# Residual sums of the second token half in small tiles, scaled from there; two low parts made on GpSimd

## The chip, the core and the metric

The kernel runs on one core of a Trainium2 chip. The metric is the device time of one execution in microseconds (us). The core has a matrix engine (PE, with its weight loads as PEld), a vector engine (DVE), a scalar engine (ACT) and a general engine (POOL, GpSimd); SP only issues DMAs here. Each works through its own queue in order; semaphores tie the queues together.

## The reference, cut to what matters

One decoder layer for 1024 new tokens of one sequence and 8 single tokens of running sequences, 1032 tokens in all, width 1024. The two recurrent mixers are left out here; o_a and y are their outputs, 1024 wide each, and gate and val have 2816 columns each:

```python
h = rmsnorm(x, w['norm1_w'])
proj = h @ w['w_in']
...
x = x + jnp.concatenate([o_a, y], axis=-1) @ w['w_out']
h = rmsnorm(x, w['norm2_w'])
gate, val = jnp.split(h @ w['w_up'], 2, axis=-1)
gate, buf_f_new = causal_dwconv(gate, buf_f, w['ffn_conv_w'], w['ffn_conv_b'])
x = x + (jax.nn.silu(gate) * val) @ w['w_down']
```

All of it is float32. The change concerns the sum behind `w_out`, the second norm's weight and the first products with `w_up`.

## The kernel before

Everything is kept transposed: features on the 128 partitions, tokens along the row. A float32 product is made from three reduced-precision ones: each operand is split into a high part (a cast to the type fp32r, on ACT) and a low part (the operand less its high part, usually on DVE), and PE adds high x high, high x low and low x high.

**Output projection** (`out_job`, L1199). The 1032 tokens stand in two halves (`hf`) of 516, each in two quarters (`c`) of 258 (`QW`). The result is `xh[hf][m]`, eight rows of tiles m of 128 features; `xpair` holds two of them in one tile. Jobs named o8 and o12 do one half of the contraction for all tokens, then o0 and o4 the other, first for half 0, then for half 1 (`o0.*.1`, `o4.*.1`). Each product is 12 matmuls into a PSUM bank, emptied by an addition on DVE (L1234). In the last job of a half (`last`, the o4 jobs) the sum is complete. `final` (L1244) then stores it to DRAM (`x1_d`, for the last residual), squares it on ACT and adds the square on POOL to `rst`, from which the second norm's factor comes. For half 1, `weigh` (L1256) multiplies the finished row of tiles, in place, by the norm's weight `n2`. It is put off by 28 ticks; a tick is one matmul traced. The token's own factor is applied to half 1 only behind the up projection (L1498, L1507).

**Sets** (`set_of`, L1328). The up projection uses seven products instead of eight on quarters of the operands (the Strassen-Winograd form): weights in feature halves 1 and 2 and in gate and value columns, activations a1, b1 (quarters 0 and 1, rows 0 to 3) and a2, b2 (quarters 0 and 1, rows 4 to 7). The seven operands p1 to p7 of a half are its set: p1 = a1, p2 = a2, p4 = b2, p5 = b1 - b2, p6 = p5 less a1, p3 = p6 plus a2, p7 = a1 - b1. `comb` (L1356) makes the sums in two pieces on DVE or POOL. `put` (L1345) casts the high part on ACT (L1352) and subtracts for the low part on DVE (L1353). Plain operands are taken in two pieces of 128x516, sums in one of 128x1032.

**Up projection** (`ups`, L1526; `Up`, L1445). For each of 22 blocks of 128 columns there are 14 products of 12 matmuls: in block 0 the seven of half 0, then the seven of half 1 (`FIRST`); in the others alternating (`ORDER`). Products p1, p7 and p3 (named ua) use a pool of three PSUM banks; the others (ub) use one of four. Their evictions are p1 L1464 and p5 L1472 (ACT), p6 L1468, p2 L1484, p4 L1492, p7 L1476 and p3 L1504 (DVE). p4's waits until p7 has been added up; p3's until POOL has done L1477 and L1478 behind p7. `set_norm` sums the squares over the partitions with a matmul (n2ms) and works out the factor (`rstd_of`, L736 to L739). Weight sums of the next block are made by POOL (L1422), its splits are L1441 (ACT) and L1442 (DVE).

**What sets the order.** PE runs in the order of the code (`manual_schedule` for PE). Everything else is traced between PE's matmuls: `after(n, f)` runs f n ticks later and `spread(pieces, n)` one piece every n ticks. The queues of the other engines are ordered by the planner of the tile framework: an instruction traced earlier goes first among those that it reckons ready. A tile that is allocated takes a buffer of its tag when one is free. The tags of `TAGS` (L42) that matter are hT (16 buffers of 1032), big (10 of 1056), x5 (5) and us (10 of 258). During the output projection hT holds its inputs; big holds the eight residual tiles. The tag us holds the squares, the evicted products and the norm's scratch.

The lists of the sets are made from these lines:

```python
after(4, lambda: spread(set_of(1), 4))
after(93, lambda: (set_norm(1, 0), set_norm(1, 1)))
for _ in ups(0, [(name, i) for i in range(2) for name in FIRST]):
    tick()
```

Of the kernel before, what the change touches and what calls it, by code (L numbers as in the profile page):

```python
# [8 lines left out]
F32 = mybir.dt.float32  # L9
# [41 lines left out]
def hybrid_layer(  # L51
# [104 lines left out]
    def col(name, i=0):  # L156
        c = vlay[name] + i
        return vcol[:, c:c + 1]
# [83 lines left out]
    def after(n, work):  # L242

        later.append([n, work])
# [954 lines left out]
    def out_job(r0, m, halves=(0, 1), last=False):  # L1199
        def load():  # L1200
            w = wload(w_out[0, r0 * P:(r0 + 4) * P, m * P:(m + 2) * P], 4, 2 * P,
                      kept=(r0 // 4 * 4 + m // 2, halves[0]) if len(halves) == 1 else None)
            rm = {(8, 4): 0, (8, 6): 2, (12, 4): 4, (12, 6): 6}.get((r0, m))
            return w, [(rm + i, residual_load(rm + i)) for i in range(2)] if rm is not None else []

        def run(loads):
            w, res = loads
            at_ = AHEAD.get((r0, m, halves[0]))
            if at_ is not None:
                if at_[0] == 8:  # L1210
                    mix_ahead(8)
                    mix_ahead(12)
                else:
                    if at_[0] < 8:
                        mix_ahead(at_[0])
                    spread(ahead[at_[0]], at_[1])
            whole(r0)
            hi, lo = mixes[r0]
            if r0 == 8:
                for hf in range(2):  # L1220
                    xpair[hf][m // 2] = tl("big", "x1")[:, :NT].rearrange("p (i t) -> p i t", i=2)
                    for i in range(2):
                        xh[hf][m + i] = xpair[hf][m // 2][:, i, :]
            for i in range(2):
                for hf in halves:
                    for c in range(2):
                        cs, ts_ = slice(c * QW, (c + 1) * QW), slice((2 * hf + c) * QW, (2 * hf + c + 1) * QW)
                        ps = turn("mm", r0 < 8 or m > 2)[:, :QW]
                        yield from steps(w, i * P, (i + 1) * P, hi, lo, ts_, ps)
                        x_ = xh[hf][m + i][:, cs]  # L1230
                        if r0 == 8:
                            evicted[0] = A.copy(x_, ps)
                        else:
                            evicted[0] = V.tensor_tensor(x_, x_, ps, op=ALU.add)  # L1234
                        if last:
                            final(m + i, x_, ts_)
                            if hf and c:
                                after(28, lambda m=m + i: weigh(m))
                        yield True
                if res:  # L1240
                    spread(residual(*res[i]), 8)
        job(f"o{r0}.{m}" + (f".{halves[0]}" if len(halves) == 1 else ""), load, run)

    def final(m, x_, ts_):  # L1244

        SP.dma_start(x1_d[m][:, ts_], x_)
        if m == 0:
            A.activation(rst[:, ts_], x_, AF.Square)
        else:
            sq = tl("us", "n2sq")  # L1250
            A.activation(sq, x_, AF.Square)
            G.tensor_tensor(rst[:, ts_], rst[:, ts_], sq, op=ALU.add)

    weighed = set()

    def weigh(m):  # L1256

        A.activation(xh[1][m], xh[1][m], AF.Copy, scale=col("n2", m))
        weighed.add(m)

    turns = [0]

# [65 lines left out]
    def set_of(i):  # L1328


        ts_ = slice(2 * i * QW, 2 * (i + 1) * QW)
        xp = [t.rearrange("p i (c t) -> p i c t", c=2) for t in xpair[i]]

        def block(h1, c):
            return [xp[2 * h1 + q][:, :, c, :] for q in range(2)]

        a1, b1, a2, b2 = block(0, 0), block(0, 1), block(1, 0), block(1, 1)

        def norm(h1):
            for m in range(4 * h1, 4 * h1 + 4):  # L1340
                x_ = xh[i][m]
                V.scalar_tensor_tensor(x_, x_, col("n2", m), rst[:, ts_], op0=ALU.mult, op1=ALU.mult)
                yield

        def put(name, src, tag):  # L1345
            hi, lo = tl(tag, "uh", F32R), tl(tag, "ul", F32R)
            hq, lq = quads(hi[:, :NT]), quads(lo[:, :NT])
            usets[i][name] = hq, lq
            n = 4 // len(src)
            for q, t in enumerate(src):  # L1350
                rows = slice(q * n, (q + 1) * n)
                A.copy(hq[:, rows], t)  # L1352
                V.tensor_tensor(lq[:, rows], t, hq[:, rows].bitcast(F32), op=ALU.subtract)  # L1353
                yield

        def comb(out, eng, x_, y_, op):  # L1356
            t = quads(tl("x5", "sm")[:, :NT])
            out.append(t)
            for q in range(2):
                eng.tensor_tensor(t[:, 2 * q:2 * q + 2], x_[q], y_[q], op=op)  # L1360
                yield

        def two(t):
            return [t[:, 0:2], t[:, 2:4]]

        s_ = []
        if i == 0:
            yield from norm(0)
            yield from norm(1)
            yield from put("p2", a2, "big")  # L1370
            yield from put("p4", b2, "e")
            yield from comb(s_, V, b1, b2, ALU.subtract)
            yield from comb(s_, V, two(s_[0]), a1, ALU.subtract)
            yield from comb(s_, G, a1, b1, ALU.subtract)
            yield from comb(s_, G, two(s_[1]), a2, ALU.add)
            while "o0.6.1" not in done:
                yield
            yield from put("p1", a1, "hT")
            yield from put("p6", [s_[1]], "hT")
            up_load(0)  # L1380
            yield from put("p5", [s_[0]], "hT")
            yield from put("p7", [s_[2]], "hT")
            yield from put("p3", [s_[3]], "big")
            up_split(0, 0)
            after(76, lambda: up_split(0, 1))
        else:
            d_ = []
            yield from comb(d_, G, a1, b1, ALU.subtract)
            yield from put("p1", a1, "hT")
            while len(weighed) < KT:  # L1390
                yield
            yield from put("p2", a2, "big")
            yield from comb(s_, V, b1, b2, ALU.subtract)
            yield from comb(s_, V, two(s_[0]), a1, ALU.subtract)
            yield from comb(s_, G, two(s_[1]), a2, ALU.add)
            yield from put("p4", b2, "big")
            yield from put("p6", [s_[1]], "hT")
            yield from put("p5", [s_[0]], "hT")
            yield from put("p7", d_, "hT")
            yield from put("p3", [s_[2]], "big")  # L1400

    ORDER = ("p1", "p6", "p5", "p7", "p2", "p4", "p3")
# [271 lines left out]
```

## Time and profile before

| | us |
|---|---|
| median of 3 runs (1722.42 to 1723.65) | 1723.61 |
| the profiled execution, its own time | 1728.11 |
| its span, first to last instruction | 1726.4 |
| PE busy | 1692.1 |
| DVE busy | 1083.8 |
| ACT busy | 776.1 |
| POOL busy | 483.9 |
| granted clock of PE (1 is full) | 0.999 |

The times are from the start of the span. The first product of the up projection starts at 1002.97. A group's row has line, engine, operation, tiles and shapes, count, then busy us and mean ns, then the idle time of the engine before them and what ended it. In a timeline row stand start, length, engine, line and operation; a bracket at the end gives the idle time just before and what ended it. In a row of busy time by stretches each engine has us and, in brackets, instructions, in the order PE, PEld, DVE, ACT, POOL; then come the granted clock, the DMA share and GB/s. A matmul row's length overlaps with the next one's, so PE's pace is read from the count. The names in rows are those of the code; x is a tile of the residual, x_d the DRAM tensor x1_d, uh and ul the high and low part of a set, sm a sum of the sets.

### The profile page before, as it was taken

To read this page: it belongs to the slowest core of one execution; us is meant where nothing else is said; L and a number is where in the kernel's file an instruction comes from. 1 tells how busy PE (TensorE), PEld (TensorE's weight loads), DVE (VectorE), ACT (ScalarE), POOL (GpSimd) and SP (SyncE) were. 2 spreads that over 40 slices of the span, in tenths; PEclk is the share of its full clock that TensorE was granted. 3 is DMA by queue.
4 is the path that set the end of the run, shared out by engine and by line. 5 is a ranking of instruction groups with operands and counts; after the bars stand their busy time and mean duration, and the time that the engine had idled before them with its cause. 6 is when DMAs were issued, how large, how long until landed. Compare 5 with 4: busy or idle time off the path is not lost. (4 is left out here: it accounts for less than half of the span.)

```text
span 1726.4 us, 38305 instructions
## 1 busy us (share of the span) xinstructions
PE 1692.1 (98%) x16056; PEld 1648.5 (95%) x16056; DVE 1083.8 (63%) x1970; ACT 776.1 (45%) x1424; POOL 483.9 (28%) x501
## 2 busy tenths in 40 slices
PE   7999999999999999999999989999999999999997
PEld 7899998999999999999999989999999999999997
DVE  6667756565575565566746787666667667544445
ACT  7567675444355354455333464333343334211114
POOL 2102131120120121111222266666666664000002
PEclk9999999999999999999999999999999999999999
DMA  5354334543433424435448722222222226422212
GB/s 169 66 129 110 107 92 141 152 133 109 120 112 115 121 89 141 121 98 164 137 130 265 230 62 88 97 75 74 74 75 87 78 95 212 169 68 95 81 56 99
DMA packets 251001, 200.22 MB, mean 116 GB/s; under 512 B 48030, under 2 KB 222614, under 8 KB 250811
## 3 DMA queue, kind: packets, MB, share of 16 engines
q1 hardware_dynamic: 250538, 197.67, 37.7%
q8 instruction: 126, 2.06, 0.5%
q14 instruction: 49, 0.39, 0.1%
q0 software_dynamic: 288, 0.10, 0.0%
HBM read 155.16 MB, written 46.95 MB: 117 GB/s over the span
## 5 line engine op out<-in xcount | busy, mean ns | idle before, releaser
L93 PE MATMUL mm<-hl,wh 128*128 128x344 f32 x1248 | 404.5, 324 | 0.5 <-issue 0.5
L93 PE MATMUL mm<-hh,wh 128*128 128x344 f32 x1248 | 404.4, 325 | 0.0
L93 PE MATMUL mm<-hh,wl 128*128 128x344 f32 x1248 | 401.3, 322 | 0.0
L93 PEld LDWEIGHTS mm<-hl,wh 128*128 128x128 f32 x1248 | 234.9, 188 | 4.7 <-issue 4.2
L93 PEld LDWEIGHTS mm<-hh,wh 128*128 128x128 f32 x1248 | 235.0, 188 | 3.1 <-issue 2.5
L93 PEld LDWEIGHTS mm<-hh,wl 128*128 128x128 f32 x1248 | 235.1, 188 | 1.9 <-issue 1.8
L199 ACT CAST wh<-ws 128x1024 fp32r<-128x1024 f32 x96 | 100.6, 1048 | 246.4 <-PE dn L93 132.2
L93 PE MATMUL ub<-uh,wh 128*128 128x258 f32 x704 | 200.1, 284 | 5.2 <-DVE fext L1492 2.7
L93 PE MATMUL ub<-uh,wl 128*128 128x258 f32 x704 | 198.9, 283 | 0.0
L93 PE MATMUL ub<-ul,wh 128*128 128x258 f32 x704 | 198.3, 282 | 0.0
L93 PE MATMUL dn<-al,wh 128*128 128x256 f32 (+1 forms) x640 | 180.3, 282 | 0.0
L93 PE MATMUL dn<-ah,wh 128*128 128x256 f32 (+1 forms) x640 | 180.2, 282 | 0.0
L93 PE MATMUL dn<-ah,wl 128*128 128x256 f32 (+1 forms) x640 | 179.7, 281 | 0.0
L201 DVE TENSOR_TENSOR wl<-ws,wh 128x1024 fp32r<-128x1024 f32 x88 | 115.5, 1312 | 94.8 <-ACT wh L199 93.9
L93 PE MATMUL ua<-uh,wh 128*128 128x258 f32 x528 | 149.5, 283 | 1.3 <-DVE val L1504 1.3
L93 PE MATMUL ua<-uh,wl 128*128 128x258 f32 x528 | 149.3, 283 | 0.1
L93 PE MATMUL ua<-ul,wh 128*128 128x258 f32 x528 | 148.8, 282 | 0.0
L93 PE MATMUL mm<-mh,wh 128*128 128x258 f32 x512 | 145.4, 284 | 0.1
L93 PE MATMUL mm<-ml,wh 128*128 128x258 f32 x512 | 145.1, 283 | 0.0
L93 PE MATMUL mm<-mh,wl 128*128 128x258 f32 x512 | 144.7, 283 | 0.0
L93 PEld LDWEIGHTS ub<-uh,wh 128*128 128x128 f32 x704 | 133.0, 189 | 6.4 <-DVE fext L1492 2.9
L1442 DVE TENSOR_TENSOR wl<-wt,wh 128x512 fp32r<-128x512 f32 x88 | 89.9, 1040 | 77.0 <-ACT wh L1441 77.0
(367 smaller groups left out, 3947.7 us busy)
## 6 DMA issues: line engine op xcount, KB each, us to landing
ws<-in_w_in_dram SPq DMA_DIRECT2D x52, 512.0 KB
ws<-in_w_up_dram SPq DMA_DIRECT2D x44, 512.0 KB
ws<-in_w_out_dram SPq DMA_DIRECT2D x24, 512.0 KB
act_d<-val SPq DMA_DIRECT2D x22, 516.0 KB
al<-act_d SPq DMA_DIRECT2D x22, 516.0 KB
ws<-in_w_down_dram SPq DMA_DIRECT2D x22, 512.0 KB
ml<-mix_d SPq DMA_DIRECT2D x48, 172.0 KB
csb<-cs_d SPq DMA_DIRECT2D x32, 256.0 KB
```

The lines of the kernel that those rows point to most:

```text
L93: PE.matmul(out, lhsT, rhs, start=start, stop=stop)
L199: A.copy(wh[:, :n], ws[:, :n])
L201: V.tensor_tensor(wl[:, :n], ws[:, :n], wh[:, :n].bitcast(F32), op=ALU.subtract)
L1442: V.tensor_tensor(lo[:, cs], sums[name], hi[:, cs].bitcast(F32), op=ALU.subtract)
```

## The change

In the o4 jobs of half 1 the last addition on DVE no longer writes back into the residual tile, but into a new tile of the tag us (128x258). The store, the square and, at once, the scaling by `n2` read it. The scaling writes the residual tile; it is now one instruction for each quarter, sixteen in all, without the 28 ticks. `weighed` counts sixteen. In the set of half 1, p7's operand is put first, right behind its difference, into big, and p2 goes to hT; the low parts of p7 and p5 are made by POOL; the sum for p3 is made behind p5, where it was made ahead of p4.

```diff
                         x_ = xh[hf][m + i][:, cs]
+                        y_ = tl("us", "x1") if last and hf else x_
                         if r0 == 8:
                             evicted[0] = A.copy(x_, ps)
                         else:
-                            evicted[0] = V.tensor_tensor(x_, x_, ps, op=ALU.add)
+                            evicted[0] = V.tensor_tensor(y_, x_, ps, op=ALU.add)
                         if last:
-                            final(m + i, x_, ts_)
-                            if hf and c:
-                                after(28, lambda m=m + i: weigh(m))
+                            final(m + i, y_, ts_)
+                            if hf:
+                                A.activation(x_, y_, AF.Copy, scale=col("n2", m + i))
+                                weighed.append(m + i)
                         yield True
...
-    weighed = set()
-
-    def weigh(m):
-
-        A.activation(xh[1][m], xh[1][m], AF.Copy, scale=col("n2", m))
-        weighed.add(m)
+    weighed = []
...
-        def put(name, src, tag):
+        def put(name, src, tag, eng=V):
...
-                V.tensor_tensor(lq[:, rows], t, hq[:, rows].bitcast(F32), op=ALU.subtract)
+                eng.tensor_tensor(lq[:, rows], t, hq[:, rows].bitcast(F32), op=ALU.subtract)
...
             yield from comb(d_, G, a1, b1, ALU.subtract)
+            yield from put("p7", d_, "big", G)
             yield from put("p1", a1, "hT")
-            while len(weighed) < KT:
+            while len(weighed) < 2 * KT:
                 yield
-            yield from put("p2", a2, "big")
+            yield from put("p2", a2, "hT")
             yield from comb(s_, V, b1, b2, ALU.subtract)
             yield from comb(s_, V, two(s_[0]), a1, ALU.subtract)
-            yield from comb(s_, G, two(s_[1]), a2, ALU.add)
             yield from put("p4", b2, "big")
             yield from put("p6", [s_[1]], "hT")
-            yield from put("p5", [s_[0]], "hT")
-            yield from put("p7", d_, "hT")
+            yield from put("p5", [s_[0]], "hT", G)
+            yield from comb(s_, G, two(s_[1]), a2, ALU.add)
             yield from put("p3", [s_[2]], "big")
```

## The prediction

> **What bounds the kernel now.** I read the page's busy shares first, then the busy time in stretches around the place of the change, then the waits of PE in that place, then the chain of waits, and last the queues of DVE, ACT and POOL in order of time.
>
> ```profile
> PE 1692.1 (98%) x16056; PEld 1648.5 (95%) x16056; DVE 1083.8 (63%) x1970; ACT 776.1 (45%) x1424; POOL 483.9 (28%) x501
> ```
>
> PE is the bound of the whole, so a change to the other engines is worth only the PE stalls that it removes. The change sits where the output projection ends and the up projection begins. In the busy time by stretches (per engine: busy us, then instructions) this place stands out:
>
> ```profile
> 980.00:1000.00 20.00, 20.00 (x169) 20.00 (x169) 16.95 (x28) 15.56 (x27) 8.60 (x10) 1.00 0.66 200
> 1000.00:1010.00 10.00, 9.68 (x81) 9.50 (x80) 6.53 (x9) 6.41 (x15) 9.55 (x9) 1.00 0.39 122
> 1010.00:1020.00 10.00, 8.30 (x60) 7.22 (x58) 9.59 (x12) 5.80 (x10) 7.11 (x6) 1.00 0.08 25
> 1020.00:1030.00 10.00, 6.46 (x49) 6.06 (x50) 9.01 (x17) 5.85 (x13) 2.26 (x2) 1.00 0.01 2
> ```
>
> At full pace PE runs 169 matmuls in 20 us, 0.118 us each; from 1000 to 1030 it runs 190, where 30 / 0.118 = 254 would fit. The 64 that are missing are 7.5 us; by busy time the idle is 0.32 + 1.70 + 3.54 = 5.6 us. The granted clock is 1.00 throughout, so this is waiting. DVE is busy 9.6 and 9.0 of 10 us in the two bad stretches. All that PE waits for from 985 to 1060:
>
> ```profile
> PE ub L93 <- DVE fext L1492: 2.7, 1, 2.7
> PE ub L93 <- ACT us L1472: 1.3, 1, 1.3
> PE ua L93 <- DVE val L1504: 1.3, 1, 1.3
> PE ub L93 <- DVE us L1468: 0.4, 1, 0.4
> PE ub L93 <- DVE nt L737: 0.4, 1, 0.4
> PE ub L93 <- DVE x L1234: 0.3, 1, 0.3
> PE n2ms L93 <- POOL n2r L1252: 0.3, 1, 0.3
> ```
>
> Every row but the last names an instruction that empties a PSUM bank: PE doesn't wait for the operand sets of the second half, it waits because evictions stand behind the making of those sets in the queues of DVE and ACT. (The six others sum to 5.4 us, the idle time of these stretches; the 1.3 us of L1504 falls after them, in the next weight block.) The chain of waits says which:
>
> ```profile
> 1019.57 3.43 DVE ul L1353 x3
> ...
> 1023.51 1.56 POOL val L1477
> 1025.07 0.71 POOL us L1478
> ...
> 1025.81 0.42 DVE val L1504
> 1026.23 0.68 DVE nt L737 x2
> ...
> 1026.96 1.70 PE ub L93 x12
> ```
>
> Three low parts run in a row on DVE, then the eviction of p7 (L1476), two POOL subtractions that need it, the eviction of p3 and the norm's first step, which frees the bank that p5 of the second half goes into.
>
> **Removed: ACT's wait for the stores.** The scaling at L1258 overwrites the tile that a DMA is still storing. The queues, ACT first, then DVE:
>
> ```profile
> 990.83 0.73 ACT L1258 ACTIVATE x<-x,vcol 128x516 f32<-128x516 f32 x1 [1.13 <-DMA x_d<-x]
> ...
> 1003.36 0.73 ACT L1258 ACTIVATE x<-x,vcol 128x516 f32<-128x516 f32 x1 [2.25 <-DMA x_d<-x]
> ```
>
> ```profile
> 986.34 0.42 DVE L1234 TENSOR_TENSOR x<-x,mm 128x258 f32<-128x258 f32 x1
> ...
> 993.68 0.75 DVE L1234 TENSOR_TENSOR x<-x,mm 128x258 f32<-128x258 f32 x2
> ...
> 996.97 1.74 DVE L1234 TENSOR_TENSOR x<-x,mm 128x258 f32<-128x258 f32 x5
> ...
> 1004.94 1.03 DVE L1442 TENSOR_TENSOR wl<-wt,wh 128x512 fp32r<-128x512 f32 x1 [2.30 <-ACT wh L1441]
> ```
>
> ACT stands 2.25 us before 1003.36; the weight cast behind it is late, and DVE stands 2.30 us for that cast at 1004.94, with four evictions of the output projection and all of the second set queued behind it. With the sum in a small tile of its own the scaling has no store to wait for, so DVE goes on up to 2.3 us earlier from there. What is late next is DVE's own work. The other waits of this sort lie where PE doesn't stall, and I count nothing for them.
>
> **Added on ACT.** Eight scalings become sixteen of half the width:
>
> ```profile
> L1258 ACT ACTIVATE x<-x,vcol 128x516 f32<-128x516 f32 x8 | 5.8, 723 | 5.1 <-DMA x_d<-x 4.6 <-ACT n2sq L1251 0.5
> L1251 ACT ACTIVATE n2sq<-x 128x258 f32<-128x258 f32 x14 | 5.5, 412 | 3.7 <-DVE x L1234 3.7
> ```
>
> A half-width activation took 0.412 us, so 16 x 0.412 = 6.6 us against 5.8: 0.8 us more, spread from 985 to 1004, covered by the 5.1 us of waiting that go; without that cover it would be 0.8 us at most. The delay of 28 ticks (28 x 0.118 = 3.3 us) before each scaling goes too; ACT and DVE were never out of other work for it, so nothing is counted.
>
> **Moved: two low parts from DVE to POOL.** In the groups of 1000 to 1030 (DVE) and 984 to 1030 (POOL):
>
> ```profile
> L1353 DVE TENSOR_TENSOR ul<-sm,uh 128x1032 fp32r<-128x1032 f32 x4 | 4.7, 1221 | 0.0
> ```
>
> ```profile
> L1360 POOL TENSOR_TENSOR sm<-x 128x516 f32<-128x516 f32 x2 | 2.5, 1235 | 0.6 <-ACT x L1258 0.6
> ```
>
> DVE loses 2 x 1.22 = 2.44 us, and these are two of the three at 1019.57 (p6, p5, p7 in the trace's order). With the 2.3 us above, p7's eviction could come 4.7 us earlier. POOL writes no fp32r tile in this trace; from below the price is DVE's 1.22 us, from above four times the 0.71 us of the 258-wide POOL row of the chain, 2.84 us. I take twice the 516-wide row, 2.47 us each, the same shape but for the width. So POOL gets 4.9 us. Its queue where that has to fit:
>
> ```profile
> 1009.29 1.75 POOL L1422 TENSOR_TENSOR wt<-wt,ws 128x512 f32<-128x512 f32 x1
> ...
> 1014.83 1.09 POOL L1252 TENSOR_TENSOR n2r<-n2r,n2sq 128x258 f32<-128x258 f32 x1
> 1017.22 1.19 POOL L1360 TENSOR_TENSOR sm<-sm,x 128x516 f32<-128x516 f32 x1 [1.30 <-DVE sm L1360]
> ```
>
> POOL ends at 1018.41 and then stands until 1023.51. The set that p7 reads needs only rows 0 to 3 of the residual, so its low part can run ahead of the weight sums (L1422), which belong to the next block. The sum p3 reads (L1360, the 1.19 us and its fellow) now comes after p5's low part. So POOL is through at 1018.41 - 1.30 (its wait, as DVE is earlier) + 4.9 = 1022.0. Then L1477 and L1478, 0.71 us each if nothing blocks them, end at 1023.4 against 1025.78: 2.4 us earlier. That is the least, with POOL's chain starting no sooner than before; where it starts sooner by what ACT and DVE gain, DVE's 4.7 us are the bound. I take 3.1, nearer to POOL's end, since POOL is busy 9.55 of 10 us from 1000. The bank of p5 is free that much earlier. The stalls before it (0.3, 0.4, 1.3 and 2.7 us) are within DVE's 4.7 and shrink to little. The norm's sum on PE (n2ms) waits for POOL's add at 1014.83: p7's low part comes in ahead of it (+2.5), the first half of p3's sum goes out (-1.2), and the squares are 2.3 us earlier, so this stays within 1 us of before. The 0.4 us behind L737 mostly stays.
>
> **The rest.** p7's tiles now come from the pool of the residual and p2's from that of the projection's inputs. The former is free when p7 is made, the latter when PE has left the projection, where p1's tiles already waited for the same: nothing, and if p2's cast did stand for it, ACT has 5.1 us of waits less to set against it. SP issues the same sixteen stores from other tiles in the same order.
>
> **The sum.** 3.1 us at the bank of p5, and 0.9 of the 1.3 us that PE stands in the next block, where DVE arrives up to 4.7 us earlier and PE 3.1: 4.0 us. The profiled execution took 1728.11 us (span 1726.4), 4.5 over the median of 1723.61; 1724.1 of its own time, 1719.6 against the median.
>
> **Rivals.** *All stalls go.* POOL is not in the way, as the planner runs both low parts while it waits, and PE gains what it is idle in these stretches to the full pace, 7.5 us, and the 1.3 us: 1723.6 - 8.8 = 1714.8. For it: POOL stands 5.1 us before 1023.51. Against it: p5's low part has to wait for sums that come late in the set.
>
> *POOL and DVE block each other.* At 1008.99 two half-size low parts took 2.60 us where a full-size one, with as many elements, takes 1.22, while a weight sum on POOL took 1.75 us at 1009.29:
>
> ```profile
> 1008.99 2.60 DVE L1353 TENSOR_TENSOR ul<-x,uh 128x516 fp32r<-128x516 f32 x2
> ```
>
> From 1005 to 1016 the two engines' instructions with two operands in SBUF look serial. Then each moved part costs both engines 2.47 us instead of 1.22, 2.5 us for the two, and the gain is 4.0 - 2.5 = 1.5: 1722.1. For it: POOL is busy 9.55 of 10 us from 1000. Against it: POOL is idle from 1018.41 to 1023.51, where p5's part fits. [...]
>
> *Evictions wait for their new tiles: slower.* The small tiles share 10 buffers with the squares. A product needs two, so a buffer comes round after five products, 5 x 12 x 0.118 = 7.1 us. A sum keeps its buffer until the store has landed: from 986.76, the end of an eviction, to 990.83, 4.1 us. At PE's pace that is enough. But DVE empties in bunches: of the five at 996.97 the last starts at 998.3, and the sum five before it left at 994.4, landing at 998.5. Where the bunches are a little tighter the wait that ACT had stands on DVE itself, where evictions, splits and sets all queue behind it. It decides once evictions run more than 3 us (7.1 - 4.1) behind PE. Two such waits of up to 4.1 us, less DVE's 2.44 that are saved, give 5.8 more at worst, 3 to 6 with POOL's blocking: about 1728. For it: the bunch of five. Against it: it is ACT's waits that bunch the evictions, and those go.
>
> *The change doesn't do what it says.* DVE, ACT and POOL are ordered by a planner; it may put the evictions behind the sets as before, and the stalls only change their names: 1723.6.
>
> **Chances.** The forecast 0.46 (own range 1717 to 1722), all stalls 0.13, blocking 0.19, slower by the tiles 0.15, no effect 0.07. The range cuts into the two outer cases and leaves out less than half of each: 1715.0 to 1727.5. A measurement tells 0.2% (3.4 us) from no change, so faster means below 1720.2: seven tenths of the forecast (0.32) and the first rival, 0.45; slower than 1727.1 is most of the third, 0.13; the rest, 0.42, is within.
>
> **What would show it.** Right: no ACT wait for the stores; DVE doing two large low parts fewer after 1003, POOL two of about 2.5 us; in the stretches from 1000 to 1030 some 25 to 30 matmuls more; p5's wait for L737 or p3's for L1504 as the longest stall left. Wrong: DVE waiting at L1234 for a store or for POOL's adds, n2ms waiting over 1 us for POOL, or DVE's low parts stretched to twice 1.22 us. A wait for the sets themselves on PE would overturn the reading that only evictions matter.

## The result

The changed kernel takes 1733.85 us (median), the kernel before 1723.63 us on the same chip: ratio 1.0058, 95% interval 1.0045 to 1.0071. That is 10.2 us slower, outside the predicted range and on the other side of no change.

The profiled execution of the changed kernel took 1734.45 us, with a span of 1732.7. The one of before that the prediction worked from was 4.5 us over its median, so another execution of the kernel before, unchanged, stands beside it (1722.92 us, expected and told first among the runs below). The span of each is cut at two matmuls, the first of the up projection and the first of the down projection, by their starts in the timeline of PE:

| us | first up product at | from there to the first down product | from there to the end |
|---|---|---|---|
| before, as predicted from | 1002.97 | 453.43 | 270.0 |
| before, the other execution | 997.79 | 453.24 | 270.17 |
| changed | 999.44 | 455.41 | 277.85 |

So there are two places. The changed kernel lost some 2.1 us in the up projection, where the change was made and a gain was forecast. The larger part, 277.85 - 270.1 = 7.7 us, it lost 450 us later, at the start of the down projection, which the prediction doesn't mention. (Where the first up product starts scatters by several us between executions of one kernel; nothing is read from it.)

**Profile after.** First the busy shares of the changed kernel, then its busy time by stretches:

```profile
PE 1698.1 (98%) x16056; PEld 1654.6 (95%) x16056; DVE 1084.4 (63%) x1968; ACT 777.6 (45%) x1432; POOL 489.8 (28%) x503
```

```profile
1000.00:1010.00 10.00, 10.00 (x83) 9.80 (x82) 8.62 (x11) 6.25 (x16) 9.92 (x8) 1.00 0.16 55
1010.00:1020.00 10.00, 5.65 (x24) 4.35 (x24) 10.00 (x11) 5.31 (x9) 7.88 (x7) 0.76 0.00 0
1020.00:1030.00 10.00, 9.21 (x69) 9.00 (x69) 7.01 (x18) 4.58 (x10) 4.08 (x3) 0.90 0.01 2
...
1450.00:1460.00 10.00, 5.24 (x44) 5.04 (x42) 8.26 (x12) 6.43 (x7) 4.13 (x4) 0.95 0.97 393
1460.00:1470.00 10.00, 8.92 (x57) 8.93 (x58) 6.68 (x9) 2.11 (x2) 0.00 (x0) 0.71 0.79 274
```

PE has 6.0 us more busy time for the same 16056 matmuls: in several of these rows the granted clock is below 1, where in the execution that the prediction worked from it was 1.00 throughout. The same two late stretches of the kernel before have 86 matmuls each at 1.00. PE's waits in the changed kernel, first from 985 to 1060, then (last row) from 1440 to 1480, where the kernel before has none that is listed:

```profile
PE n2ms L93 <- POOL n2r L1254: 3.1, 2, 2.7
PE ua L93 <- DVE val L1501: 1.3, 1, 1.3
PE ub L93 <- DVE nt L737: 0.8, 1, 0.8
PE ub L93 <- DVE us L1465: 0.7, 1, 0.7
PE ua L93 <- DVE ul L1350: 0.6, 1, 0.6
...
PE dn L93 <- DVE wl L201: 5.8, 1, 5.8
```

Lines have moved: L1501, L1465 and L1473 to L1475 are before's L1504, L1468 and L1476 to L1478; L1254 is POOL's add of squares, L1350 the low parts. The waits for L1492 (2.7) and L1472 (1.3) are gone as forecast, but 3.1 us for the norm's sum stand in their place: 6.5 us in all against before's 6.7.

**The down projection.** DVE's queue there, the changed kernel first, then the kernel before (L1155 is the low part of an activation that is loaded for the down projection, L201 that of its weights, L356 the convolution at the end of the last up block):

```profile
1453.30 1.23 DVE L1155 TENSOR_TENSOR al<-al,ah 128x1032 fp32r<-128x1032 f32 x1
...
1454.80 1.31 DVE L356 SCALAR_TENSOR_TENSOR fcv<-fext,vcol,fcv 128x1048 f32<-128x1048 f32 x1
...
1457.59 2.30 DVE L1155 TENSOR_TENSOR al<-al,ah 128x1032 fp32r<-128x1032 f32 x1
1459.81 1.21 DVE L201 TENSOR_TENSOR wl<-ws,wh 128x1024 fp32r<-128x1024 f32 x1
```

```profile
1454.88 1.22 DVE L201 TENSOR_TENSOR wl<-ws,wh 128x1024 fp32r<-128x1024 f32 x1
...
1456.38 1.31 DVE L356 SCALAR_TENSOR_TENSOR fcv<-fext,vcol,fcv 128x1048 f32<-128x1048 f32 x1
...
1459.16 2.33 DVE L1155 TENSOR_TENSOR al<-al,ah 128x1032 fp32r<-128x1032 f32 x1
```

Before, the first weights are split ahead of the convolution and a later activation; after, behind both, 4.9 us later by the start of the span, though PE's first down product comes some 1.5 us earlier. And PE's queue in the changed kernel at that point:

```profile
1454.97 0.28 PE L93 MATMUL dn<-al,wh 128*128 128x256 f32 x1
1461.08 0.58 PE L93 MATMUL dn<-ah,wl 128*128 128x256 f32 x1 [5.83 <-DVE wl L201]
1461.46 0.41 PE L93 MATMUL dn<-ah,wh 128*128 128x256 f32 x1
1461.67 0.41 PE L93 MATMUL dn<-al,wh 128*128 128x256 f32 x1
```

After the 5.8 us the matmuls come 0.21 us apart instead of 0.12: half the clock (granted 0.50 from 1460 to 1464), for some 20 of them. 5.8 + 20 x 0.1 = 7.8 us, about the 7.7 us of the table.

Ahead of the split a load has become late. When SP issues the activations of the down projection, before (the first fence) and after (the second); then when ACT casts the fourth, before and after:

```profile
1440.14 0.50 SPq L1564 DMA_DIRECT2D al<-act_d  x1
...
1442.55 1.77 SPq L1564 DMA_DIRECT2D al<-act_d  x2
```

```profile
1440.98 0.42 SPq L1561 DMA_DIRECT2D al<-act_d  x1
1446.65 0.43 SPq L1561 DMA_DIRECT2D al<-act_d  x1
```

```profile
1449.72 1.06 ACT L1154 CAST ah<-al 128x1032 fp32r<-128x1032 f32 x1 [0.19 <-DMA al<-act_d]
```

```profile
1451.21 1.05 ACT L1154 CAST ah<-al 128x1032 fp32r<-128x1032 f32 x1 [3.72 <-DMA al<-act_d]
```

The activations go into hT. In the last up block the products of both halves alternate in the order p1, p6, p5, p7, p2, p4, p3. Before, set 1's p7 lay in hT and its two buffers came free with the fourth pair of products; after, p2 lies there, and they come free with the fifth. So the fourth load is issued some 3 us later, and the first weights' split stands behind more of DVE's other work. That the planner orders it so because it reckons with the late load is inferred; no run shows the planner's reckoning.

**The up projection.** POOL's queue in the changed kernel, then DVE's:

```profile
997.57 2.42 POOL L1350 TENSOR_TENSOR ul<-sm,uh 128x1032 fp32r<-128x1032 f32 x1 [0.47 <-ACT uh L1349]
...
1012.34 3.28 POOL L1254 TENSOR_TENSOR n2r<-n2r,n2sq 128x258 f32<-128x258 f32 x3
1015.58 1.64 POOL L1357 TENSOR_TENSOR sm<-sm,x 128x516 f32<-128x516 f32 x1
1019.34 3.34 POOL L1350 TENSOR_TENSOR ul<-sm,uh 128x1032 fp32r<-128x1032 f32 x1 [2.12 <-ACT uh L1349]
1022.64 0.73 POOL L1474 TENSOR_TENSOR val<-us,us 128x258 f32<-128x258 f32 x1
```

```profile
1018.03 2.37 DVE L1350 TENSOR_TENSOR ul<-sm,uh 128x1032 fp32r<-128x1032 f32 x2
1020.32 0.41 DVE L1473 TENSOR_TENSOR us<-us,ua 128x258 f32<-128x258 f32 x1
...
1024.11 0.42 DVE L1501 TENSOR_TENSOR val<-us,ua 128x258 f32<-128x258 f32 x1 [2.92 <-POOL us L1475]
```

DVE has two low parts of sums ahead of p7's eviction (L1473) instead of three: p7's and p5's are gone, but p3's, which came behind the eviction, has moved ahead of it. POOL makes p5's low part before the two subtractions behind that eviction, and DVE stands 2.9 us for them. The last add for the norm's sum ends at 1015.62, 16.2 us after the first up product; before it was 1014.83 + 1.09 - 1002.97 = 13.0, and 13.3 in the other execution. PE waits for that, and from 1016 to 1022 it has half the clock (granted 0.50).

### The profile page after: what moved, and what is told of

It is laid out like the page before. It is cut to its first block, busy times and chain, and to the rows that moved or that the text cites. A ratio compares the mean times of both kernels' runs of the same rounds, so it can differ in the third digit from the quotient of the medians.

```text
span 1732.7 us, 38321 instructions
## 1 busy us (share of the span) xinstructions
PE 1698.1 (98%) x16056; PEld 1654.6 (95%) x16056; DVE 1084.4 (63%) x1968; ACT 777.6 (45%) x1432; POOL 489.8 (28%) x503
## 5 line engine op out<-in xcount | busy, mean ns | idle before, releaser
L201 DVE TENSOR_TENSOR wl<-ws,wh 128x1024 fp32r<-128x1024 f32 x88 | 115.4, 1312 | 95.1 <-ACT wh L199 94.5
L1601 DVE TENSOR_TENSOR x<-x,dn 128x256 f32<-128x256 f32 (+1 forms) x160 | 67.1, 421 | 110.0 <-PE dn L93 110.0
```

The source lines that it names most:

```text
L201: V.tensor_tensor(wl[:, :n], ws[:, :n], wh[:, :n].bitcast(F32), op=ALU.subtract)
L1601: V.tensor_tensor(xT[m + i][:, cs], xT[m + i][:, cs], ps, op=ALU.add)
```

## The experiments

Each was timed on one chip together with the kernel before; a ratio is to that.

**The kernel before, unchanged.** No edit.

> The kernel before, unchanged, for a second profile: its first profile was 4.5 us over its median and reached the first product of the up projection at 1002.97 where the others reach it at 997 to 1000.4. Theory: that lead is a matter of the execution, not of the change; a second profile reaches it at 997 to 1000.5, the first block (first product to p7 of half 1) then takes about 27 us instead of 25.5, and the whole is 1723 to 1724. Rival: it reaches it at 1003 again and the block takes 25.5; then the change itself makes the part ahead shorter.

1722.92 us, by the table as long as the other in both later parts. Its wait of 2.7 us for L1492 is the same as before's, yet this time the clock fell behind it:

```profile
1020.00:1030.00 10.00, 9.95 (x68) 9.67 (x69) 8.97 (x21) 4.28 (x7) 3.89 (x9) 0.83 0.00 0
```

**Only the pools of p2 and p7**, in the kernel before:

```diff
-            yield from put("p2", a2, "big")
+            yield from put("p2", a2, "hT")
...
-            yield from put("p7", d_, "hT")
+            yield from put("p7", d_, "big")
```

> The kernel before with one edit: in the set of half 1, p7 goes to the pool big and p2 to hT, both made at the same place as before. Theory (pools): p2 is the fifth product of a block and p7 the fourth, so two buffers of hT are held one pair of products (24 matmuls, 2.9 us) longer at the end of the last block; the fourth activation of the down projection is loaded later, the planner then puts the first weight split of that projection behind six other instructions of DVE, and PE stands there for about 6 us and starts again at half clock: 8 us more than before, about 1731.5 us, with the stall at 1455 to 1465 and nothing changed at 1000 to 1030. Rival (shifted times): the stall at 1455 comes from the loads arriving at other times because the first block ended elsewhere; then this kernel is within 1 us of before, about 1723.6.

1734.28 us, ratio 1.006 (1.0043 to 1.0077): as slow as the whole change. At the down projection PE waits the same 5.8 us for L201, and the part to the end takes 277.34 us: the swap alone has the 7 us there. From the first up to the first down product it takes 455.96 us, 2.6 more than before. PE's longest wait in the up projection:

```profile
PE ub L93 <- DVE x L1234: 2.8, 1, 2.8
```

In this execution ACT stood 3.9 us for a store of the residual at 1001.32 (2.25 at that place before), DVE as long for the weight cast behind it, the eviction L1234 came late, and the clock granted from 1000 to 1010, where PE's wait lies, was 0.83. Whether the swap has a part in that isn't shown.

**The whole change without the swap** (those two lines back), and the same with the norm's sum later (`after(125, ...)` for `after(93, ...)` ahead of `set_norm(1, 0)`); then the later sum alone, with the swap.

> The kernel after with the pools as before: p7 (still first in the set, low part still on POOL) in hT, p2 in big. Theory (pools): 8 us less than after, about 1726; the stall at the start of the down projection is gone; PE's wait for POOL's adds (n2ms) and the half clock behind it stay, since nothing of them depends on the pools, unless p7's cast now waits for PE to leave the projection. Rival (shifted times): the stall at 1455 stays and the time stays at 1733 to 1734.

> The kernel after with both: the pools as before and n2ms 32 matmuls later. Theory: both losses gone, 1721 to 1722.5, 1 to 2.5 us under before, as what is left of the first block's stalls is shorter. Rival (serial DVE and POOL): the first block is as long as in before or longer, 1724 to 1726.

> The kernel after with the second norm's sum over the partitions of half 1 (n2ms) 32 matmuls later in PE's order (125 ticks instead of 93). Theory (POOL's adds): PE no longer reaches n2ms before POOL's last add, the 3.1 us wait and the 20 or so matmuls at half clock go, 3 to 5 us less than after, about 1729.5; the stall at 1455 stays. Rival (serial DVE and POOL): POOL and DVE are what ends the block, the wait only changes its name (a bank not emptied) and the time is within 1 us of after.

Without the swap 1727.60 us (1.0021, 1.0012 to 1.0030), and with the later sum 1725.42 (1.0011, 1.0001 to 1.0021): the wait at the down projection is 0.3 us or none, and the part from the first down product takes 271.2 and 270.6 us. With the swap and the later sum 1734.71 (1.0063, 1.0048 to 1.0078). The gain expected of the later sum without the swap, 1 to 2.5 us under the kernel before, did not come; its rival (1724 to 1726) did. In the up projection the waits mostly change their names: that part takes 454.98 us without the swap, 453.58 with the later sum as well, and 454.76 with the later sum and the swap (455.41 in the changed kernel). Without the swap PE waits for a low part itself. ACT casts p7's operand 4.7 us behind the first up product there, in the changed kernel 3.0 us ahead of it, and p1's low part comes behind that; that p7's tiles in hT are the reason was not tested. With the later sum and the swap PE waits for two banks:

```profile
PE ua L93 <- DVE ul L1350: 3.3, 2, 3.0
```

```profile
PE ub L93 <- DVE fext L1481: 4.2, 2, 2.2
```

**The start of the down projection mended in part.** The first weights are traced at the twelfth product of the last up block, so that the planner meets them earlier; in the kernel with only the pools swapped, in the changed kernel, and in the changed kernel with 24 matmuls more (into a bank that is overwritten) ahead of the norm's sum, to keep PE busy there:

```diff
+            if n == 11 and j == FT - 1:
+                first_down.append(wload(w_down[0, 0:RND * P, 0:2 * P], RND, 2 * P))
```

> The pools swapped as in b_pools, and the first weights of the down projection loaded and split two thirds into the last block, as the code traces them there instead of behind it. The fourth activation is as late as in b_pools. Theory (order): what costs is the place of the weight split on DVE, not the late load; PE stands less than 1 us at the start of the down projection, and the time is 1724 to 1726 against 1734.3 of b_pools. Rival (late load): PE stands 4 to 6 us for the fourth activation's parts instead, and the time stays at 1731 or more.

> The kernel after, whole, with the first weights of the down projection loaded and split early as in b_pools_dn. Theory (order): 7.5 to 8.5 us less than after, 1725 to 1726.5; what is left over the time before is the change's own effect on the first block, 1.5 to 2.5 us. Rival (late load): within 2 us of after. If it comes out under 1723 the first block has gained as forecast, and only the far end spoiled it.

> a_dn with 24 matmuls of p1's operands more, written to the bank of n2ms and overwritten by it, right ahead of n2ms: 24 x 0.118 = 2.8 us of work more for PE, where it stood 2.7 us for POOL's add. Theory (clock): the wait is filled, the granted clock stays at 1.00 between 1010 and 1025, and the 20 matmuls at half clock become full ones: 2 us less than a_dn although PE does more. Rival (no room): the wait isn't where PE would stand in every execution, the matmuls come on top: 1 to 2.8 us more than a_dn.

1730.48 us (1.0041, 1.0027 to 1.0054), 1730.57 (1.0040, 1.0026 to 1.0053) and 1731.56 (1.0044, 1.0029 to 1.0059): less than half of the loss is back. Now the first weights are in time and the fourth activation's low part is what stands behind the convolution. The row of the changed kernel with the early weights:

```profile
PE dn L93 <- DVE al L1155: 3.8, 1, 3.8
```

The filled PE (its profile is of its longest execution, 1734.92 us) has no half clock from 1010 to 1020 (granted 1.00), and waits 0.3 us for the norm's sum, but then 1.5 and 2.3 us for banks and has 0.86 from 1020 to 1030. Filling in gained nothing, as one would expect if DVE and POOL set the length of the stretch: 455.64 us up to the first down product, 455.38 without the filling.

**The start mended in full.** Beside the weights the first four activations' loads are traced at that place too, and the convolution's end goes behind the fourth one's low part on DVE:

```diff
+                first_acts.extend(act_load(k) for k in range(RND))
+        if j == FT - 1:
+            with tc.issue_after(split_last[0].ins):
+                up_close(j, us_[0])
```

> The changed kernel with its pools as changed, but the first weights and the first four activations of the down projection are traced at the twelfth block of the last pair, and the last pair's tail on DVE is put behind the fourth activation's low part. Theory 'the swap costs by order alone' (set 1's p2 keeps its two tiles of the projection's pool until late, the fourth activation comes late, and the planner puts it behind the tail): with the order mended PE's wait at the first product of the down projection falls from 5.8 us to under 1, the tail from that product to the end from 277.9 to 270-271 us, and the kernel from 1733.9 to 1724-1727. Rival 'the buffers themselves come too late' (the load, not the order, is late): the wait stays at 3 us or more, now for a load, and the time at 1729-1731, as where only the weights were put earlier (1730.6).

1726.84 us, ratio 1.002 (1.001 to 1.003). No wait of PE is listed from 1440 to 1480, and the part to the end takes 269.93 us. The fourth activation's cast in this kernel, and DVE's queue behind it:

```profile
1451.73 1.05 ACT L1154 CAST ah<-al 128x1032 fp32r<-128x1032 f32 x1 [3.94 <-DMA al<-act_d]
```

```profile
1453.92 1.22 DVE L201 TENSOR_TENSOR wl<-ws,wh 128x1024 fp32r<-128x1024 f32 x1
1455.06 1.23 DVE L1155 TENSOR_TENSOR al<-al,ah 128x1032 fp32r<-128x1032 f32 x1
...
1456.87 1.30 DVE L356 SCALAR_TENSOR_TENSOR fcv<-fext,vcol,fcv 128x1048 f32<-128x1048 f32 x1
```

The cast starts 3.7 us ahead of the first down product, in the changed kernel 3.6, before 6.7: the load is as late as in the changed kernel, and it costs nothing. So it is the order on DVE that costs the 7.7 us. The late load comes with that order, and costs nothing by itself. What is left is 3.1 us over the kernel before: 2.1 in the up projection (455.35 against 453.24), the rest ahead of it, where executions scatter.

**The change's other parts, each alone and together**, in the kernel before, pools and order of the sets as they were. The edits are those lines of the change's diff: small tiles and scaling at once; `eng=G` for the low parts of p5 and p7; both.

> The kernel before with the sums of the second half in small tiles and the scaling from there at once, and nothing else: pools, order of the sets and low parts as before. Theory of the prediction: ACT's wait for the stores goes, DVE gets up to 2.3 us and p5's bank is free earlier; 1720.5-1722.5. Rival 'serial DVE and POOL' (the stage from the first product of the weight block to p7 of the second half is bound by DVE and POOL together, 26-27 us whatever ACT does): 1723-1725, that stage within 1 us of 25.5-27.0. Rival 'evictions wait for small tiles': DVE waits at the eviction for a store, 1726-1728.

> The kernel before with the low parts of the second half's p5 and p7 on POOL instead of DVE, and nothing else. Theory of the prediction: DVE loses 2.4 us, POOL gets 4.9, the sums behind p7's eviction end about 2.4 us earlier; 1721-1722. Rival 'serial DVE and POOL': POOL's chain (p7's low part, weight sums, norm's sum) gets longer by what DVE loses, PE stands for the norm's sum or for the sets instead; 1723.5-1726, the stage 26-28 us.

> The kernel before with the small tiles, the scaling at once and the two low parts on POOL: the whole change less its new order of the sets and its swap of pools. Theory of the prediction: 1719-1721, its sum of 4.0 us less what the order brings. Rival 'serial DVE and POOL': 1723-1726, the stage 26-28 us, with PE waiting 2-3 us for POOL's norm sum or for a low part. In both no wait of 3 us or more at the first product of the down projection, since p2 stays where it was.

1723.23 us (0.9998, 0.9990 to 1.0007), 1723.94 (0.9999, 0.9989 to 1.0008) and 1724.64 (1.0004, 0.9995 to 1.0012): nothing measurable, alone or together. The new order of the set isn't among them. From the first up to the first down product they take 453.06, 454.13 and 454.85 us. The last row of the queue of DVE, then POOL's, in the kernel with both:

```profile
1022.07 0.42 DVE L1501 TENSOR_TENSOR val<-us,ua 128x258 f32<-128x258 f32 x1 [5.29 <-POOL us L1475]
```

```profile
1009.58 3.23 POOL L1357 TENSOR_TENSOR sm<-sm,x 128x516 f32<-128x516 f32 x2
1014.93 5.73 POOL L1350 TENSOR_TENSOR ul<-sm,uh 128x1032 fp32r<-128x1032 f32 x2 [2.12 <-ACT uh L1349]
```

DVE is through early and stands 5.3 us for the two low parts that POOL took over. With the small tiles alone, DVE no longer stands for weight casts (4.7 us in two waits before), but 2.9 us for casts of the set; and PE's wait for p6's bank is 3.2 us in place of 0.4, as that eviction comes behind three low parts on DVE.

**The two subtractions on DVE.** They follow p7's eviction; if POOL's low part ahead of them is what DVE stands for, DVE can do them itself. The first edit puts them there for half 1 of the tokens (`self.i`); but the ones in question belong to half 0, whose products come first in this block, so these four kernels moved two others.

```diff
+            sub = V if self.i and not self.j else G
-            G.tensor_tensor(self.val[:, self.at(1)], self.f, self.u3, op=ALU.subtract)
-            G.tensor_tensor(self.u2, self.f, self.u2, op=ALU.subtract)
+            sub.tensor_tensor(self.val[:, self.at(1)], self.f, self.u3, op=ALU.subtract)
+            sub.tensor_tensor(self.u2, self.f, self.u2, op=ALU.subtract)
```

> The kernel before with the two low parts on POOL, and the two subtractions behind p7's eviction of the second half, in this one block alone, on DVE instead of POOL. Theory 'the low part stands ahead of the subtractions': with the low parts alone DVE stands 2.9 us for POOL's second subtraction, because POOL makes p5's low part (2.7 us) first; on DVE they follow p7's eviction at once, so PE's wait of 2.3 us for the norm's first step falls to under 0.7 and the kernel from 1723.9 to 1721-1722.5. Rival 'the stage is bound elsewhere' (DVE and POOL block each other, or the clock takes it back): PE's other waits grow by as much, 1723.3-1724.5.

> The kernel before with those two subtractions on DVE in this one block, and nothing else; the control for the run with the low parts on POOL. In the kernel before POOL is free when p7 is evicted, takes 1.56 + 0.74 us for them beside a low part on DVE, and DVE stands 1.0 us. Theory 'the low part stands ahead': there is no low part on POOL here, so little is to be had: PE's wait for the norm's step stays under 0.7, the bank's row (2.7 us for DVE's fext) moves by at most 1 us; 1722.7-1723.7. Rival 'the subtractions on POOL were the bound all along': 2 us or more, 1721-1722, as much as with the low parts moved.

> Small tiles and low parts on POOL, as before the swap and the new order, with the two subtractions of this block on DVE. Theory 'the low part stands ahead of the subtractions': DVE stood 5.3 us for POOL, PE 2.2 us for the norm's step; both go, and the kernel falls from 1724.6 to 1722-1723. Rival 'bound elsewhere': 1724-1725, with the 3.2 us for the eviction of p6 grown or a half-clock stretch longer.

> The changed kernel with the start of the down projection mended, and the two subtractions of this block on DVE. In the run without this PE waited only 0.3 us for the norm's step, since it had come late by 2.7 us for the norm's sum and a stretch at half clock. Theory 'in the whole change the norm's sum and the clock bind, not the bank': nothing to be had, 1726-1727.5. Rival 'the low part of p5 binds there too': 2 us faster, 1724-1725.

1725.24 us (1.0008, 0.9999 to 1.0017), 1722.66 (1.0000, 0.9992 to 1.0009), 1726.87 (1.0018, 1.0009 to 1.0027) and 1727.01 (1.0020, 1.0011 to 1.0029). In all of them DVE stands for POOL as long as without the edit (2.9, 1.0, 5.3 and 2.9 us), so they say nothing on the question. With the right half (`sub = G if self.i or self.j else V`):

> The kernel before with the two low parts on POOL, and the two subtractions behind p7's eviction of the first half in this block (the ones for which DVE stood 2.9 us; the four runs before had moved those of the second half's p7 instead) on DVE. Theory 'the low part stands ahead of the subtractions': DVE goes from p7's eviction on without a wait, the norm's first step comes about 2.5 us earlier, PE's wait of 2.3 us for it falls to under 0.7, and the kernel from 1723.9 to 1721-1722.7. Rival 'the stage is bound elsewhere': PE waits for p5's or p3's low part on POOL or for another bank instead, 1723.3-1724.5.

> The kernel before with those two subtractions of the first half on DVE, and nothing else: the control. Theory 'the low part stands ahead': POOL is free there, the subtractions took 1.56 + 0.74 us beside a low part on DVE, DVE stood 1.0 us; on DVE they are 2 x 0.41 ahead of p3's low part, so the bank behind the second half's fext (PE's 2.7 us) moves by under 1 us either way: 1722.9-1724.2. Rival 'the subtractions on POOL were the bound all along': as much as with the low parts moved, 1721-1722.7.

1725.45 us (1.0009, 1.0000 to 1.0018) with the low parts on POOL, 1723.45 (1.0001, 0.9992 to 1.0010) without. The wait went, and the time did not. The profile with the low parts on POOL is of its longest execution (1728.85 us). The subtractions on DVE beside POOL's low parts; then the low parts, one row for both; then the same subtractions in the control, where POOL is idle:

```profile
1020.58 2.08 DVE L1478 TENSOR_TENSOR val<-us,us 128x258 f32<-128x258 f32 x1
1022.59 2.58 DVE L1479 TENSOR_TENSOR us<-us,us 128x258 f32<-128x258 f32 x1
1025.09 0.41 DVE L1493 TENSOR_TENSOR fext<-us,ub 128x258 f32<-128x258 f32 x1
```

```profile
1019.71 5.17 POOL L1353 TENSOR_TENSOR ul<-sm,uh 128x1032 fp32r<-128x1032 f32 x2 [3.01 <-ACT uh L1352]
```

```profile
1020.85 0.41 DVE L1478 TENSOR_TENSOR val<-us,us 128x258 f32<-128x258 f32 x1
1021.19 0.41 DVE L1479 TENSOR_TENSOR us<-us,us 128x258 f32<-128x258 f32 x1
```

An instruction of 0.41 us took 2.08 and 2.58: each ends 0.3 to 0.4 us, about its own length, behind the end of a low part on POOL (1019.71 + 5.17 / 2 = 1022.3, and 1024.9). So beside POOL's instructions of 2.6 us DVE did not subtract two tiles in SBUF, while it did evict a bank (one operand in SBUF): in the changed kernel L1473 takes its 0.41 us at 1020.32, with POOL's low part running from 1019.34 to 1022.68. PE's wait for the bank behind L1493 grew from 2.7 us before to 5.1 in this kernel, and 24 matmuls 0.21 us apart followed, at half clock (granted 0.71 from 1020 to 1030, the wait included). The theory that the subtractions merely stood in the wrong queue fell. The runs fit a stretch that is bound by the work with two operands in SBUF of DVE and POOL taken together, which gets longer when the slower engine does more of it (a low part of a sum took 2.42 us on POOL in the changed kernel, 1.22 on DVE before); that nothing else binds there isn't shown.

No kernel here is faster than the kernel before by more than the measurement's uncertainty.

## Why the prediction was wrong

**The rest** is the step that failed. It priced the swap of the pools at nothing, as p2's tiles are free in time where they are made. It did not ask when they come free again. Their two buffers of hT are held one pair of products longer, to the very end of the up projection, where the down projection's activations wait for them. The swap alone makes the kernel as slow as the whole change (1734.28), 7.2 us of it at the down projection (277.34 against 270.1); with DVE's order mended there, the 7.7 us of the changed kernel are back (277.85 to 269.93). The prediction followed each queue only near the change. The forecast gain near the change, 4.0 us, failed as well; its terms follow.

**Removed: ACT's wait for the stores.** The mechanism was right: no such wait is left in the changed kernel. The gain was not there: the small tiles alone gave 1723.23 against 1723.70, since part of DVE's wait (three evictions stood behind the late cast, not the four that were counted) came back behind other casts and p6's eviction fell behind low parts of the set.

**Added on ACT** was too small, 2.2 us instead of 0.8, but as forecast no wait of PE is seen to come of it. The scalings in the changed kernel (groups, ACT from 984 to 1012) are longer than the 0.412 us taken, 16 x 0.498 = 8.0 us instead of 6.6. DVE still stands 4.3 us for a weight cast behind them (4.7 before), where PE doesn't wait:

```profile
L1239 ACT ACTIVATE x<-x,vcol 128x258 f32<-128x258 f32 x14 | 7.0, 498 | 0.0
```

**Moved: two low parts from DVE to POOL.** The duration was right: 2.42 us where 2.47 was taken, and 3.34 for the one that started, at 1019.34, beside low parts on DVE (1018.03 to 1020.40). That L1477 and L1478 would end 2.4 us earlier was wrong: counted from the first up product, L1478's end came at 22.8 us before (1025.77 - 1002.97), 23.2 in the other execution, and at 24.6 after (1023.34 + 0.73 - 999.44). The step let p5's low part run in POOL's free time from 1018.41; in fact ACT casts p5's high part behind p3's, which waits for POOL's own sum (L1357, until 1017.22), so the low part starts at 1019.34 and runs straight across p7's eviction. The norm's sum, which was to stay within 1 us, comes 3.2 us later (2.9 against the other execution).

**The sum** of 4.0 us was not there in any part: the small tiles measured -0.5 us, the low parts +0.2 and both together +0.9, none of them clear of zero. With the new order of the set as well, and only the swap taken out, it was 3.9 us slower (1727.60). That kernel also has p7 first in the pool hT, so the price of the order by itself wasn't measured.

**The rivals.** *POOL and DVE block each other* named what the run with the subtractions on DVE shows, 2.08 and 2.58 us for 0.41. How much of the missing 4.0 us it took, beside the order of POOL's queue, wasn't separated; at 2.5 us it would have left a gain that no run shows. *Evictions wait for their new tiles* was the slower side, and not what happened: DVE's wait at that eviction for POOL's adds is 0.8 us in the changed kernel, and the small tiles alone aren't slower. *All stalls go* fell. *The change doesn't do what it says* came nearest in time for the small tiles and the low parts (1723.2 to 1724.6), though both were carried out; the whole change less its swap was slower. A loss far from the change was on no list.

**What would show it.** The signs named as wrong were there: DVE waiting at that eviction for POOL's adds (0.8 us), PE 3.1 us for the norm's sum, and PE waiting for a set itself (0.6 us here, 3.3 without the swap), which the prediction had taken as not binding. From 1000 to 1030 PE ran 176 matmuls where 190 were before and 215 to 220 forecast; but the first up product comes at another time in each execution. Over 30 us from that product the rows have 172 in the changed kernel, and 188 and 176 in the two executions of the kernel before. The 25 to 30 more did not come; that there were clearly fewer isn't shown. No sign looked behind 1060.

Still open is the last 2 us in the up projection of the changed kernel. It goes with waits of about the same length as before, plus stretches at half clock, which come in some executions of one kernel and not in others, as the repeated kernel shows (granted 1.00 and 0.83 from 1020 to 1030). Making the norm's sum later shortened that part by 0.7 us with the swap and by 1.4 without, in one profile each; how much of the 2 us is clock and how much the norm's sum wasn't separated further.

## What to carry to other kernels

When a tile changes its pool, follow both buffers to their last reader in the last pass of the loop, and name what is allocated there next; the price may stand hundreds of us away, and it can be one of order alone. Ahead of moving work from DVE to POOL, ask whether what is left on DVE has both operands in SBUF: if so, the two engines can end up taking turns, as they did here (0.41 us became 2.08 and 2.58), and the work gets no shorter. A stall of PE can be dearer than its length: here some 20 matmuls behind the 5.8 us ran at half clock, 2 us more.

## What the runs showed of the hardware

With the low parts on POOL and the two subtractions on DVE, a DVE subtraction of two tiles in SBUF ended only behind POOL's subtraction of two tiles in SBUF (0.41 us became 2.08 and 2.58), while in the changed kernel a DVE addition that reads a PSUM bank and an SBUF tile kept its 0.41 us beside one.

The granted clock fell to 0.50 behind waits of at most 2.7 us. The changed kernel in steps of 2 us, behind waits of 0.6 and 2.7 us with two matmuls between them:

```profile
1014.00:1016.00 2.00, 1.05 (x3) 0.62 (x4) 2.00 (x3) 0.01 (x1) 2.00 (x3) 0.79 0.00 0
1016.00:1018.00 2.00, 1.55 (x5) 1.06 (x4) 2.00 (x3) 0.74 (x1) 1.22 (x1) 0.50 0.00 0
...
1020.00:1022.00 2.00, 2.00 (x11) 2.00 (x11) 1.15 (x3) 1.55 (x4) 2.00 (x1) 0.50 0.04 8
1022.00:1024.00 2.00, 2.00 (x19) 2.00 (x18) 0.00 (x0) 0.13 (x1) 2.00 (x3) 1.00 0.00 0
```

In one execution of the kernel before a wait of the same 2.7 us left the clock at 1.00 (from 1020 to 1030), in the other 0.83 over the same 10 us followed it. What decides between the two was not shown.
